# Tile-outermost order for a convolution layer, with its LayerNorm spread between the matmuls

## Chip, cores and metric

The program runs on the 8 cores of one Trainium2 chip. Each core works through two sequences of an encoder on its own; the cores exchange nothing. The metric is the device time of the slowest core in microseconds (us).

Some executions fall into a second, slower state in which the cores of one die, or of both, show a lower granted clock in the records; these last some per cent longer whatever the kernel.

Engines are named as in the profile: PE is the matrix engine (TensorE), PEld its weight loads, DVE is VectorE, ACT is ScalarE, POOL is GpSimd, SP the engine that issues most transfers.

## The reference

Four layers of mixer and MLP, each behind an RMS norm and added to x. The mixers are pooling, convolution, Fourier, pooling. Only the second one and the norm of the MLP behind it matter here:

```python
def conv_module(h, w_in, dw, dw_bias, ln_g, ln_b, w_out):
    val, gate = jnp.split(h @ w_in, 2, axis=-1)
    v = val * jax.nn.sigmoid(gate)                              # GLU, (B, S, 1024)
    v = lax.conv_general_dilated(v, dw[:, None, :], ...,        # depthwise over positions, width 31
        padding=((15, 15),), feature_group_count=D_CONV) + dw_bias
    mu = jnp.mean(vf, axis=-1, keepdims=True)                   # LayerNorm over the 1024 channels
    var = jnp.mean(jnp.square(vf - mu), axis=-1, keepdims=True)
    vn = (vf - mu) * lax.rsqrt(var + LN_EPS) * ln_g + ln_b
    return jax.nn.silu(vn) @ w_out

    # in the loop over layers
    x = x + mixers[i](rms_norm(x, norm_mix[i]))
    x = x + sq_relu_mlp(rms_norm(x, norm_mlp[i]), mlp_up[i], mlp_down[i])
```

A sequence has 2048 positions, cut into 4 tiles j of 512. The 1024 channels are 8 blocks c of 128.

## The kernel before

The kernel is a program generator: Python emits instructions in program order, and a recorder finds from the memory that each one touches which semaphores it must wait for. Memory is tracked in granules:

```python
GRAN = 128
...
        for l, h in zip(lo.tolist(), hi.tolist()):
            for gi in range(l // GRAN, (h - 1) // GRAN + 1):
                s.add((name, gi))
```

Two instructions that touch one granule are ordered if one of them writes, even where their bytes differ. Each engine is handed its instructions in program order, so "what stands where" is the whole schedule. An instruction that depends on an earlier one of its own engine waits on a semaphore too (PE excepted).

The convolution layer takes a channel block at a time. GLU of block c, then v goes to DRAM and comes back in four copies that are shifted by 8 positions, then four tiles of convolution, 32 matmuls each, on four column tiles of PE. The shifted copies are read for two tiles at once:

```python
        def glu(c, j):
            ...                                   # cut: 8 + 8 matmuls into banks bg, bv
            sg = SG.next()
            self.act(sg, bg, AF.Sigmoid)
            self.tt(Vc[c % 2][:, CONV_PAD + j * TT:CONV_PAD + (j + 1) * TT], bv, sg, ALU.mult)

        def vread(c, h, b):
            sc = self.scr["v"][c % 2]
            v4 = self.buf(b, BF16, (4, L))        # L: two tiles + 8
            for sh in (0, 2, 1, 3):
                src = bass.AP(sc.tensor, sc.offset + h * HT * TT + 8 * sh, [[VW, 32], [32 * VW, 4], [1, L]])
                self.dma("sp", f"v{c % 2}{h}", (s, c), v4[32 * sh:32 * sh + 32], src, ...)

        def conv(c, j, b, late=None):
            ...
            for m in range(8):
                for q in range(4):
                    self.mm(bank[32 * q:32 * q + 32, :], DG[:, q * 8 + m, :], ..., m == 0, m == 7, skip=True)
            self.act(C, bank, AF.Identity, bias=self.vcol(f"l{li}_conv_dw_bias", c))
            ...                                   # cut: C and its square are added up on VectorE over c
        for c in range(1, DC - 2):                # channel block outermost
            if c > 1:
                build_diag(c - 1)
                for j in range(NT):
                    glu(c, j)
            ...
            for h in range(2):
                for j in range(h * HT, (h + 1) * HT):
                    conv(c - 1, j, v4[h])
                spread(c, h, v4[h])               # write v of block c, read it back
```

All of LayerNorm and the output product therefore comes at the end, when the last channel block is done, and one tile stands behind the other:

```python
        def normalize(j, upto):
            for c in range(upto):
                ...
                self.tt(t1, Cv(c, j), ACC1[:, j, :], ALU.subtract, eng="pool" if c % 2 else "dve")
                self.tt(t1, t1, ACC2[:, j, :], ALU.mult)
                self.act(SLv(c, j), t1, AF.Silu, ...)

        def out(j, mid=None):
            ...
            for kc in range(DC):
                normalize(j, kc + 1)
                for oc in range(NB):
                    self.mm(banks[oc], wk(kc, oc), SLv(kc, j), kc == 0, kc == DC - 1)
            ...                                   # cut: x += bank, square of x for the next norm
        out(0, ...)
        self.x_ready(self.nxt, 0)
        out(3)
        self.x_ready(self.nxt, 3)
        self.slots_early(s, li, 1)
        self.h_open(self.nxt)
        self.h_step(99)                           # norm roots, 16 pieces and 16 differences for the MLP
        out(1)
        self.mlp_sums(s, li)
        out(2)
        for j in (1, 2):
            self.x_ready(self.nxt, j)
```

The MLP multiplies in a recursive form, on sums and differences of input pieces: tiles 0 and 3 are the first pair. Its first matmuls need the pieces of both, and so the root of the mean square of both.

## Time and profile before

| | before |
|---|---|
| time, first four runs | median 4682.6 us (4677.8 to 4897.6) |
| the six fast runs of the comparison below | 4677.8 to 4685.2 us |
| profiled execution, slowest core | 4678.4 us |
| cores, granted clock | 4667.3 to 4678.4 us, 0.971 |
| convolution layer, first / second sequence | 288.2 / 280.7 us |
| MLP behind it | 414.2 / 414.7 us |
| MLPs elsewhere | 392.6 to 414.1 us |

The lengths of stages run from the first matmul of a stage to the first of the next. I got them by counting the trace's matmuls off against the kernel's order of instructions; each is the median of the eight cores. On two cores of each trace some matmul records are missing; a recount on the six complete cores gives the same lengths within 1 us. The cores of one execution differ, by up to 4 us in a stage of the first sequence. Differences of about 1 us in the first sequence are therefore weak evidence.

A table load is what ACT does between functions of different sets; there are 17 in the program. `arena<-scr_v` is the shifted reload of v.

### The profile page before, as it was taken

To read this page: it belongs to the slowest core of one execution; us is meant where nothing else is said; L and a number is where in the kernel's file an instruction comes from. 1 tells how busy PE (TensorE), PEld (TensorE's weight loads), DVE (VectorE), ACT (ScalarE), POOL (GpSimd) and SP (SyncE) were. 2 spreads that over 40 slices of the span, in tenths; PEclk is the share of its full clock that TensorE was granted. 3 is DMA by queue.
4 is the path that set the end of the run, shared out by engine and by line. 5 is a ranking of instruction groups with operands and counts; after the bars stand their busy time and mean duration, and the time that the engine had idled before them with its cause. 6 is when DMAs were issued, how large, how long until landed. Compare 5 with 4: busy or idle time off the path is not lost.

```text
span 4678.4 us, 66415 instructions; the slowest of 8 cores (4667.3 to 4678.4 us)
## 1 busy us (share of the span) xinstructions
PE 4326.5 (92%) x21817; PEld 1964.7 (42%) x22222; DVE 2808.9 (60%) x5132; ACT 2003.5 (43%) x3367; POOL 158.7 (3%) x194
## 2 busy tenths in 40 slices
PE   7999987799978999999989999878999799999998
PEld 3444443344433444444444444433444344444443
DVE  2776645876647854578546556356646546526565
ACT  4533435433523445544355334344434245445334
POOL 0000001100020000000000000010000000000000
PEclk9999999899988999999999999988999899999999
DMA  6366653466634665267842443533444134413443
GB/s 152 85 161 203 165 127 84 91 163 203 176 112 106 177 193 142 70 162 203 232 142 97 156 146 118 137 75 125 151 149 150 51 131 153 151 59 112 156 178 131
DMA packets 97553, 652.07 MB, mean 139 GB/s; under 512 B 9920, under 2 KB 12096, under 8 KB 50368
## 3 DMA queue, kind: packets, MB, share of 16 engines
q1 hardware_dynamic: 77056, 517.25, 31.5%
q0 software_dynamic: 20160, 130.56, 15.8%
q8 instruction: 184, 3.01, 0.3%
q14 instruction: 153, 1.25, 0.1%
HBM read 625.08 MB, written 151.13 MB: 166 GB/s over the span
## 4 chain that ended last, share of the span: by engine, by line
PE 81%; DVE 7%; DMA 4%; issue 4%; ACT 3%; SPq 0%; DVEq 0%; POOL 0%; ACTq 0%; POOLq 0%
PE ps L330 81%; DVE arena L347 5%; ACT arena L344 3%; DVE arena L355 2%; DMA outT<-arena 1%; DMA scr_v<-arena 1%; DMA arena<-xT 1%; DMA arena<-l_pool_w_in 1%; DMA arena<-scr_v 0%; DMA arena<-l_pool_w_out 0%; DMA arena<-scr_mlp 0%; SPq L368 0%; ACT L344 0%; DVEq L282 0%; POOL arena L368 0%
## 5 line engine op out<-in xcount | busy, mean ns | idle before, releaser
L330 PE MATMUL ps<-arena 128*128 128x512 bf16 (+5 forms) x21817 | 4326.5, 374 | 333.3 <-DVE arena L347 112.7
L330 PEld LDWEIGHTS ps<-arena 128*128 128x128 bf16 (+1 forms) x22222 | 1964.7, 98 | 2694.7 <-issue 489.7
L347 DVE TENSOR_TENSOR arena<-arena,ps 128x512 f32<-128x512 f32 (+1 forms) x1090 | 726.0, 683 | 901.4 <-PE ps L330 886.8
L347 DVE TENSOR_TENSOR arena<-arena 128x512 bf16<-128x512 bf16 (+4 forms) x2364 | 1167.3, 512 | 165.8 <-ACT arena L344 128.0
L344 ACT ACTIVATE arena<-arena 128x512 bf16<-128x512 f32 (+3 forms) x1206 | 811.9, 681 | 671.8 <-DVE arena L347 625.7
L344 ACT ACTIVATE ps<-ps 128x512 f32<-128x512 f32 x768 | 447.0, 582 | 1107.6 <-PE ps L330 1046.9
L344 ACT ACTIVATE arena<-ps 128x512 f32<-128x512 f32 (+2 forms) x1112 | 613.2, 596 | 613.9 <-PE ps L330 573.8
L347 DVE TENSOR_TENSOR arena<-ps,arena 128x512 f32<-128x512 f32 (+1 forms) x584 | 401.3, 688 | 598.6 <-PE ps L330 555.0
L355 DVE SCALAR_TENSOR_TENSOR arena<-arena 128x512 bf16<-128x512 f32 (+1 forms) x960 | 669.0, 714 | 84.9 <-ACT arena L344 77.5
L344 ACT ACTIVATE arena<-ps,arena 128x512 bf16<-128x512 f32 (+2 forms) x264 | 168.7, 663 | 248.7 <-PE ps L330 208.1
L368 POOL DMA_DIRECT2D arena<-l_mlp x96 | 50.9, 530 | 1730.9 <-PE ps L330 1131.3
L351 DVE TENSOR_SCALAR arena<-arena 128x512 bf16<-128x512 f32 (+1 forms) x112 | 47.0, 462 | 73.8 <-DMA arena<-xT 50.6
L347 POOL TENSOR_TENSOR arena<-arena 128x512 f32<-128x512 f32 (+2 forms) x44 | 80.4, 1837 | 252.6 <-ACT arena L344 160.8
L344 ACT ACT_TABLE_LOAD x17 | 21.8, 1283 | 22.8 <-DMA arena<-xT 14.4
L368 POOL DMA_DIRECT2D arena<-l_conv_w_in x16 | 8.4, 531 | 676.2 <-DVE arena L347 522.6
L362 DVE COPY arena<-arena 128x512 f32<-128x512 f32 (+1 forms) x12 | 4.2, 346 | 39.9 <-ACT arena L344 39.9
L368 POOL DMA_DIRECT2D arena<-l_pool_w_in x14 | 7.5, 553 | 515.2 <-PE ps L330 514.0
L365 POOL MEMSET arena<- 128x1024 bf16 (+1 forms) x6 | 4.0, 702 | 419.6 <-PE ps L330 419.6
L368 POOL DMA_DIRECT2D arena<-l_conv_w_out x4 | 2.1, 527 | 237.4 <-PE ps L330 237.4
L368 POOL DMA_DIRECT2D arena<-l_pool_w_groupT x2 | 1.1, 535 | 90.4 <-DMA arena<-xT 52.4
L368 POOL DMA_DIRECT2D arena<-l_pool_w_out x4 | 2.1, 542 | 6.1 <-PE ps L330 6.1
L368 POOL DMA_DIRECT2D arena<-l_fourier_w_out_x x2 | 1.1, 554 | 0.0
(6 smaller groups left out, 2.0 us busy)
## 6 DMA issues: line engine op xcount, KB each, us to landing
arena<-scr_mlp SPq DMA_DIRECT2D x160, 1792.0 KB, 7.2
scr_mlp<-arena SPq DMA_DIRECT2D x64, 1792.0 KB, 6.5
arena<-l_mlp POOLq DMA_DIRECT2D x96, 1024.0 KB, 9.1
arena<-scr_v SPq DMA_DIRECT2D x128, 258.0 KB, 4.9
arena<-xT SPq DMA_DIRECT2D x32, 512.0 KB, 7.8
outT<-arena SPq DMA_DIRECT2D x16, 1024.0 KB, 5.3
arena<-l_conv_w_in POOLq DMA_DIRECT2D x16, 512.0 KB, 7.0
arena<-dfts SPq DMA_DIRECT2D x8, 1024.0 KB, 8.8
```

The costliest lines, as they stand in the source:

```text
L330: self.P.add("pe", lambda e: e.matmul(out, lhsT, rhs, start=start, stop=stop, skip_group_check=skip), reads=[lhsT, rhs], writes=[out])
L344: self.P.add("act", lambda e: e.activation(out, in_, func, **kw), reads=reads, writes=[out])
L347: self.P.add(eng, lambda e: e.tensor_tensor(out, in0, in1, op), reads=[in0, in1], writes=[out])
L351: self.P.add(eng, lambda e: e.tensor_scalar(out, in0, s1, None, op0), reads=reads, writes=[out])
L355: self.P.add(eng, lambda e: e.scalar_tensor_tensor(out, in0, scalar, in1, op0, op1), reads=reads, writes=[out])
L362: self.P.add(eng, lambda e: e.tensor_copy(out, in_), reads=[in_], writes=[out])
L365: self.P.add(eng, lambda e: e.memset(ap, val), writes=[ap])
L368: return self.P.add(q, lambda e: e.dma_start(out=out, in_=in_), reads=[in_] + list(reads), writes=[out] + list(writes), chan=chan, group=g ...
```

## The change

The intent is to keep PE fed through the whole layer. The loop is turned: position tile outermost, channel block inside, in the tile order 0, 1, 3, 2. So a tile's LayerNorm and output can lie beside GLU and convolution matmuls of the next tiles. The reload works a tile at a time with four slots read ahead. The LayerNorm sums of the last two tiles are made by PE in two banks of their own, one convolution late. The sigmoid becomes a tanh, because tanh shares ACT's table with silu (sigmoid(x) = (1 + tanh(x/2))/2; the half goes into the diagonals). The roots for the MLP are prepared piece by piece, squares of tiles 1 and 2 go into the MLP. Memory is tracked at 64 bytes.

The core of the diff, cuts marked with "...":

```diff
-GRAN = 128
+GRAN = 64
...
-    M[:, lay["mask"]:lay["mask"] + 32] = np.tile(np.eye(32), (4, 1))
+    M[:, lay["mask"]:lay["mask"] + 32] = 0.5 * np.tile(np.eye(32), (4, 1))
...
-            self.act(sg, bg, AF.Sigmoid)
-            self.tt(Vc[c % 2][...], bv, sg, ALU.mult)
+            self.act(sg, bg, AF.Tanh, scale=0.5)
+            self.stt(v, sg, 1.0, bv, ALU.add, ALU.mult)
...
+        order = [(c, j) for j in (0, 1, 3, 2) for c in range(DC)]
+        def vslot(k):
+            return self.buf(v4[k % 4 // 2], BF16, (4, L), (k % 2) * (BUFSZ // 2))
...
+            if k + 4 < len(order):
+                vread(k + 4)
...
+            if onpe:                       # tiles 3 and 2
+                sq, cb = SB[0].next(), SB[1].next()
+                self.act(sq, bank, AF.Square, bias=b)
+                silus()
+                self.copy(cb, C)
+                flush()                    # sums of the convolution before this one
+                late.append((j, c, cb, sq))
...
+        def ln(j, c, lag=False):
+            C = Cv(c, j)
+            self.tt(C, C, M[slot[j]], ALU.subtract, eng="pool" if j == 0 and c % 2 else "dve")
+            self.tt(C, C, R[slot[j]], ALU.mult)
+            lagged.append((j, c))          # the silu follows later
...
+        for c in range(DC):
+            conv(16 + c)
+            if c == 0:
+                ln_stats(1)
+            if c > 1:
+                ln(1, c - 2, True)
+        Cb[2] = self.take(6, 7)
+        conv(24)
+        ln_stats(3)
...
+        for c in range(1, DC):
+            conv(24 + c)
+            if c > 2:
+                ln(3, c - 3, True)
...
+        out(1, 0)
+        ln_stats(2)
+        self.rot = Rot([ps[:, i, :] for i in range(8)])
+        for c in range(DC - 3, DC):
+            ln(3, c)
+        for oc in range(1, DC):
+            out(1, oc)
+            ln(2, oc - 1)
+        ln(2, DC - 1)
...
+        first = [h[0]] + [h[2 + 8 * k + q] for k in range(4) for q in range(2)]
+        rest = [h[1]] + [h[2 + 8 * k + q] for k in range(4) for q in range(2, 8)]
+        for oc in range(DC):
+            out(3, oc)
+            first.pop(0)()                 # root of tile 0, then its pieces
+        self.htodo = first + rest
+        self.rot.i = 0
+        for oc in range(DC):
+            out(2, oc)
+            if oc > 0:
+                self.h_step(4)             # root of tile 3, the rest
         self.mlp_sums(s, li)
-        out(2)
+        nx.lazy = [1, 2]
```

## The prediction

> **What bounds the kernel now.** I read the page's head and its chain of work first, to see which engine sets the end.
>
> ```profile
> span 4678.4 us, 66415 instructions; the slowest of 8 cores (4667.3 to 4678.4 us)
> PE 4326.5 (92%) x21817; PEld 1964.7 (42%) x22222; DVE 2808.9 (60%) x5132; ACT 2003.5 (43%) x3367; POOL 158.7 (3%) x194
> PE 81%; DVE 7%; DMA 4%; issue 4%; ACT 3%; SPq 0%; DVEq 0%; POOL 0%; ACTq 0%; POOLq 0%
> ```
>
> TensorE carries 81% of the chain, so the other 19% are what a rescheduling can win. The diff touches the convolution layer, which each core runs twice (two sequences), and the head of the MLP after it. The second view is busy time by stretch, cut at those layers. Columns: stretch; busy us and count of PE, weight loads, DVE, ACT, POOL; granted clock; DMA share; GB/s.
>
> ```profile
> 172.00:568.00 396.00, 389.06 (x1763) 175.40 (x1798) 282.43 (x526) 171.02 (x300) 14.78 (x28) 1.00 0.66 176
> 568.00:740.00 172.00, 157.89 (x1298) 72.74 (x1314) 72.60 (x107) 57.89 (x89) 2.11 (x4) 0.97 0.58 133
> 740.00:761.00 21.00, 15.42 (x239) 7.32 (x233) 9.44 (x14) 13.72 (x21) 2.49 (x2) 0.92 0.58 130
> 761.00:856.00 95.00, 63.04 (x251) 25.79 (x257) 71.53 (x90) 47.78 (x56) 30.89 (x21) 0.86 0.09 16
> 856.00:880.00 24.00, 6.09 (x16) 1.57 (x14) 22.36 (x40) 7.45 (x9) 0.00 (x0) 0.57 0.37 71
> ...
> 3094.00:3181.00 87.00, 62.26 (x250) 25.34 (x254) 67.28 (x91) 47.34 (x55) 19.25 (x14) 0.86 0.10 36
> 3181.00:3205.00 24.00, 5.80 (x15) 1.49 (x14) 22.25 (x40) 7.37 (x9) 0.00 (x0) 0.63 0.27 102
> ```
>
> The MLP (172 to 568) is full. The convolution layer is not: its output part (761 to 856) keeps PE busy 63 of 95 us, and in the 24 us from 856 it does 16 matmuls while DVE is busy 22.4 us. The third view is what PE waited for from 568 to 880.
>
> ```profile
> PE ps L330 <- ACT arena L344: 30.5, 13, 9.3
> PE ps L330 <- DMA arena<-scr_v: 15.1, 4, 7.1
> PE ps L330 <- DVE arena L355: 12.7, 4, 4.0
> PE ps L330 <- DVE arena L347: 9.5, 4, 6.2
> ```
>
> ACT is the LayerNorm's silu at the end of subtract, multiply, silu; the DMA is the shifted reload of v before the first convolution; DVE L355 are the normed MLP inputs.
>
> The floor of a layer: full matmuls start 0.216 us apart in dense stretches, and a convolution (32 matmuls, four column tiles at a time) takes 1.73 us, read from start times (the timeline gives 3.65 us for 64 of them, with entry). Going into the tiled form and out costs 0.27 us together (0.10 on the full side, up to 0.17 on the other). The order of instructions gives 1802 matmuls per layer: 778 full x 0.216 = 168, 32 convolutions x 1.73 = 55.4, about 12 round trips x 0.27 = 3.2, plus 1.5 for the MLP's first: 228 us. The first layer with MLP head takes 312 us (568 to 880), the second 305 (2900 to 3205). Lost: 84 and 77, 161 in all, 3.4% of the kernel.
>
> **What the Trainium skill says.** "ScalarE activation tables: per-element evaluation and per-set limits", section "What a function is on this engine", puts two functions of different sets one table load of 1283 ns apart. The trace agrees: 17 loads, mean 1283 ns. "TensorE: Matmul & The Clock Gate", section "What's actually happening", says the clock halves after an idle window of about 3.4 us and recovers after as much work. The stretch table agrees in direction: clock 0.57 in the head, 1.00 in the MLP; so a long wait costs a little more than itself. "GPSIMD Engine Reference" lists GpSimd's SBUF interfaces as shared with VectorE, contended by DVE instructions with two SBUF inputs. The trace fits: such 128x512 f32 TENSOR_TENSORs average 809 ns (median 692) where GpSimd subtracts alongside. "DMA: Bandwidth & Descriptors", section "How a descriptor splits into AXI transactions", has unaligned descriptors fetch bytes that they don't use; the reload packets of 2064 B average 145 ns against 108 for 2048 B rows of the input.
>
> **The change part by part.**
> 1. The loop turns from channel block outermost to position tile outermost, with whole tiles of LayerNorm and output between GLU and convolution work. All eight GLUs of tile 1 separate the first reload from its use: the 7.9 and 12.6 us before the first convolutions, and 8.2 and 3.7 inside them, should go (32 us over both layers).
> 2. The LayerNorm of a tile is now spread under GLUs or convolutions. The stalls of the output part go, except around the statistics (below). GpSimd subtracts 4 times per layer, not 16.
> 3. LayerNorm sums of tiles 2 and 3 move from DVE to PE: 32 ones-matmuls instead of 4. Added PE per layer: 28 x 0.216 = 6.0, and about 12 more changes of form (the sums stand between convolutions) x 0.27 = 3.2. Together 9.3 per layer, 18.6 in all, all on the path. New floor 238.
> 4. Sigmoid becomes tanh in the silu's set. Ln and Exp still switch, and they are now spread out: the compiled program has 29 loads against 17, 6 more per layer x 1.28 = 7.7 us of ACT. They lie beside PE work except in the two statistics between back-to-back convolutions. There, one convolution with its sums takes PE 1.73 + 0.27 + 0.43 = 2.43 us, ACT 0.57 + 0.57 + 0.72 = 1.86 (spacing of such ACTIVATEs when dense), DVE 0.34 + 2 x 0.61 = 1.56. The statistics put square, copy, load, Ln, Exp, load (0.49 + 0.49 + 1.28 + 0.62 + 0.54 + 1.28 = 4.7 us) on ACT at once; PE, which waits each time for the sums of the convolution before, loses by my step-through 0.8 us at the first and 3.0 at the second.
> 5. The MLP head. The squares of x for tiles 0 and 3 move under the outputs, tiles 1 and 2 into the MLP, and half of the pieces that the first matmuls need are made early. What is left is DVE's queue after the last convolution: 4 LayerNorm chunks x 1.22 = 4.9; outputs of tile 1 with LayerNorm of tile 2, 8 x (0.60 + 1.22) = 14.6; outputs of tile 3 with squares and 7 pieces, 8 x 0.60 + 7 x 0.335 + 7 x 0.663 = 11.8; outputs of tile 2 with 9 pieces and 16 differences, 4.8 + 6.0 + 5.4 = 16.2. With about 3 us of start and a wait of 1.8 for the root of tile 3 it ends near 52 us, while PE has 24 x 1.73 + 1 = 43. So 8 us per layer stay; in the first sequence, where the slot sum now stands on DVE behind all this (GpSimd did it before), 9.7.
> 6. Weight slabs come earlier, and dependencies are tracked at 64 B. Outside the convolution layers and the MLP after them the PE, ACT and DVE order is unchanged; I count nothing.
>
> Sum per layer: floor 238; statistics 3.8; head 8.0 or 9.7; reloads 2; clock after these waits 3; unlisted 3. That makes 259.5 and 257.8 against 312 and 305: savings of 52.5 and 47.2, together 100 us. 4683 - 100 = 4583, 2.1% less.
>
> **The rivals.**
> DMA becomes the bound of the 16 back-to-back convolutions. Each needs 532 KB in 512 packets of 1040 B, 219 GB/s at 2.43 us, while the reload reached 230 to 240 GB/s at most in 4 us samples of the trace. If a packet costs in proportion to 2064 B at 145 ns, some 85 ns with a fixed part (estimate), a convolution's reads take 2.7 us on 16 engines, and the four slots read ahead nearly absorb it. If the cost is fixed per packet, 4.6 us, 20 to 25 us per layer are lost, and the kernel ends at 4625 to 4635. For it: twice the packets for the same bytes. Against it: the written packets of 1088 B took 68 ns.
>
> DVE bounds the tail more than I reckon: each microsecond there is on the path, and in-order waits for roots can add 5 per layer; then 4593.
>
> The rewrite hides nearly everything: with only the statistics and 5 us of tail left, 4560.
>
> ACT's extra loads come where PE waits on silu: 6 per layer, at worst 15 us in all, 4598.
>
> **Range and chances.** 2% is 4589, so the estimate sits 6 us beyond the line, while my sum of leftovers (42 us over both layers) may be half or double. Range 4556 to 4628. Chances: faster by over 2% 0.52, within 2% 0.47, slower 0.01: to be slower the added PE and a DMA bound would have to exceed all that is removed.
>
> **What would show it.** In stretches of the changed kernel: the first three quarters of the convolution layer near full PE with clock 1.00 (parts 1, 2); some 56 more weight loads (3); 29 table loads (4); PE waits on ACT of 3 to 5 us per layer among the convolutions; PE idle 8 to 10 us at the MLP's first matmuls with DVE full (5); PE waits on the reload of v under 3 us per layer. Wrong if those waits exceed 10 us per layer, if the head still costs 20, or if the MLP gets longer than 394 us past its head.

## More of the kernel before

The lines that show what bounds this kernel are in the prediction. Two more of the page are wanted later. The first is a group of instructions: line, engine, operation, count, then busy us and mean ns of one, then the idle time before them. The second is a transfer: what is written from what, count, KB each, and the median us from issue to landing.

```profile
L344 ACT ACT_TABLE_LOAD x17 | 21.8, 1283 | 22.8 <-DMA arena<-xT 14.4
...
arena<-scr_v SPq DMA_DIRECT2D x128, 258.0 KB, 4.9
```

## The result, and the profile after

| | before | after |
|---|---|---|
| fast runs of the comparison | 4677.8 to 4685.2 us (6) | 4602.0 to 4608.0 us (5) |
| ratio of fast runs | | 0.9836, 95% interval 0.9823 to 0.985 |
| median of all runs, slow ones included | 4862.3 us (15) | 4652.5 us (10) |
| profiled execution, slowest core | 4678.4 us | 4603.3 us |

A ratio is the mean time of one kernel's fast runs over that of the other's from the same rounds, so it is not quite the ratio of medians. The two medians of all runs hold different shares of slow runs and say nothing about the change. The kernel is 1.6% faster. The fast runs lie 19 to 25 us above the predicted 4583, inside the range; the saving is 75 us where 100 was predicted, and that puts the change within 2%, not beyond it.

The head of the page after:

```profile
span 4603.3 us, 67285 instructions; the slowest of 8 cores (4589.4 to 4603.3 us)
...
PE 4348.3 (94%) x22278; PEld 1962.0 (43%) x22278; DVE 2775.5 (60%) x5157; ACT 2019.4 (44%) x3425; POOL 115.2 (3%) x166
...
PE 85%; DVE 6%; DMA 3%; issue 3%; ACT 3%; SPq 0%; DVEq 0%; POOL 0%; ACTq 0%; POOLq 0%
...
L346 ACT ACT_TABLE_LOAD x29 | 37.2, 1283 | 25.9 <-DMA arena<-xT 14.0
...
arena<-scr_v SPq DMA_DIRECT2D x256, 130.0 KB, 3.7
```

PE's share of the chain rose from 81% to 85%. The 56 added weight loads and the 29 table loads are as reckoned. The reload has twice the transfers at half the size.

Busy time by stretch in the first sequence, core 4 (columns as in the prediction: stretch; PE, PEld, DVE, ACT, POOL; clock; DMA share; GB/s):

```profile
568.00:740.00 172.00, 167.79 (x1266) 74.38 (x1264) 82.92 (x128) 74.96 (x111) 5.45 (x5) 1.00 0.53 115
740.00:774.00 34.00, 27.12 (x378) 10.19 (x377) 18.54 (x33) 26.75 (x41) 0.57 (x1) 1.00 0.81 166
774.00:832.00 58.00, 43.97 (x196) 19.13 (x194) 49.10 (x87) 24.62 (x34) 1.05 (x2) 0.94 0.06 9
832.00:856.00 24.00, 23.38 (x96) 9.98 (x97) 18.08 (x36) 15.35 (x28) 0.53 (x1) 0.87 0.78 187
```

The part up to 740 us is now nearly full. From 740 to 774, the last of the 16 back-to-back convolutions, PE is busy 27 of 34 us, and ACT is nearly as busy. From 774 to 832, the outputs, PE is busy 44 of 58 us beside a DVE that is busy 49. What PE waited for, 568 to 840 us (us in total, times, longest):

```profile
PE ps L332 <- DVE arena L349: 15.1, 4, 8.3
PE ps L332 <- DVE arena L364: 4.9, 3, 1.7
PE ps L332 <- ACT arena L346: 2.8, 3, 1.7
PE ps L332 <- DMA arena<-scr_v: 2.7, 1, 2.7
```

And in the second sequence, 2862 to 3130 us:

```profile
PE ps L332 <- DVE arena L349: 14.4, 4, 8.3
PE ps L332 <- DVE arena L364: 4.9, 3, 1.7
PE ps L332 <- ACT arena L346: 2.8, 3, 1.7
```

The waits for ACT's silus and for the reload are nearly gone. DVE (L349: its two-input operations; L364: the copy of a convolution for the sums on PE) has taken their place. Where the time went, by stages (median of eight cores, us):

| stage | before | after | difference |
|---|---|---|---|
| convolution + MLP, first sequence | 288.2 + 414.2 | 264.1 + 393.9 | -24.1 - 20.4 = -44.5 |
| convolution + MLP, second sequence | 280.7 + 414.7 | 261.4 + 394.8 | -19.3 - 19.9 = -39.2 |
| Fourier + MLP, first sequence | 154.4 + 403.9 | 156.4 + 401.9 | 0.0 |
| last pooling + MLP, first sequence | 136.4 + 404.1 | 139.7 + 406.5 | +5.7 |
| Fourier + MLP, second sequence | 137.1 + 401.5 | 138.9 + 400.7 | +1.1 |
| last pooling + MLP, second sequence | 129.0 + 414.1 | 130.7 + 413.7 | +1.3 |

The changed layers save 83.7 us and other layers, which the diff does not touch, lose 8.1. (The recount gives 7.3; the MLP behind the last pooling layer of the first sequence, with its scatter of 4 us, is the uncertain part.)

The same gaps placed by the prediction's own terms (gaps of PE over 0.4 us, from the start of one matmul to the start of the next, on core 4; us per layer):

| place | predicted, first / second | first | second |
|---|---|---|---|
| silus of tile 0 before its first output | 0 | 2.5 | 2.5 |
| statistics of tile 1 | 0.8 | 0.6 + 1.9 | 0.5 + 1.9 |
| statistics of tile 3 | 3.0 | 1.2 + 2.0 + 2.0 | 1.2 + 2.0 + 2.0 |
| reload of v | 2 | 3.1 | 0 |
| head: output of tile 1, root of tile 3, MLP's first matmul | 9.7 / 8.0 | 1.2 + 8.6 + 5.8 | 1.3 + 8.6 + 5.2 |
| sum | 15.5 / 13.8 | 28.9 | 25.2 |

The gaps are 13.4 and 11.4 us longer than reckoned, the layers only 8.0 and 8.0 (52.5 - 44.5 and 47.2 - 39.2): the difference is 5.4 and 3.4. Each gap holds an ordinary spacing of 0.22 us, about 2 us per layer, so of the 6 us set aside for clock and unlisted losses some 3 and 1.5 were not used. The clock's part was used: after the gaps of 8.6 and 5.8 us in the first sequence, 6 and 12 matmuls start 0.43 us apart, twice the ordinary spacing, which is worth about 4 us. The wait for the reload in the first sequence varies, from 0.8 to 1.1 us on cores 1, 3 and 5 to 2.7 on core 4.

### The profile page after: what moved, and what is told of

The parts are those of the page before. It is cut to its first block, busy times and chain, and to the rows that moved or that the text cites. A ratio compares the mean times of both kernels' runs of the same rounds, so it can differ in the third digit from the quotient of the medians.

```text
span 4603.3 us, 67285 instructions; the slowest of 8 cores (4589.4 to 4603.3 us)
## 1 busy us (share of the span) xinstructions
PE 4348.3 (94%) x22278; PEld 1962.0 (43%) x22278; DVE 2775.5 (60%) x5157; ACT 2019.4 (44%) x3425; POOL 115.2 (3%) x166
## 3 DMA queue, kind: packets, MB, share of 16 engines
q14 instruction: 157, 1.29, 0.1%
## 4 chain that ended last, share of the span: by engine, by line
PE 85%; DVE 6%; DMA 3%; issue 3%; ACT 3%; SPq 0%; DVEq 0%; POOL 0%; ACTq 0%; POOLq 0%
PE ps L332 85%; DVE arena L349 4%; ACT arena L346 3%; DVE arena L357 2%; DMA outT<-arena 1%; DMA arena<-xT 1%; DMA arena<-l_pool_w_in 1%; DMA arena<-l_pool_w_out 0%; DMA arena<-scr_mlp 0%; DMA arena<-scr_v 0%; SPq L370 0%; DVEq L283 0%; ACT L346 0%; POOL arena L370 0%; DMA scr_v<-arena 0%
## 5 line engine op out<-in xcount | busy, mean ns | idle before, releaser
L349 DVE TENSOR_TENSOR arena<-arena,ps 128x512 f32<-128x512 f32 (+1 forms) x1090 | 729.6, 684 | 903.0 <-PE ps L332 895.2
L349 DVE TENSOR_TENSOR arena<-arena 128x512 bf16<-128x512 bf16 (+4 forms) x2368 | 1127.1, 494 | 125.7 <-ACT arena L346 85.8
L346 ACT ACTIVATE arena<-arena 128x512 bf16<-128x512 f32 (+3 forms) x1188 | 780.8, 665 | 659.6 <-DVE arena L349 621.9
L349 DVE TENSOR_TENSOR arena<-ps,arena 128x512 f32<-128x512 f32 x520 | 357.6, 688 | 471.4 <-PE ps L332 426.2
L346 ACT ACTIVATE arena<-ps,arena 128x512 f32<-128x512 f32 (+2 forms) x328 | 205.6, 667 | 223.8 <-PE ps L332 196.8
L357 DVE SCALAR_TENSOR_TENSOR arena<-arena,ps 128x512 bf16<-128x512 f32 x64 | 43.6, 686 | 104.3 <-PE ps L332 83.9
L346 ACT ACT_TABLE_LOAD x29 | 37.2, 1283 | 25.9 <-DMA arena<-xT 14.0
L349 POOL TENSOR_TENSOR arena<-arena 128x512 f32<-128x512 f32 (+2 forms) x16 | 37.0, 2330 | 256.1 <-ACT arena L346 180.0
L364 DVE CAST arena<-arena 128x512 bf16<-128x512 f32 x32 | 13.7, 428 | 36.0 <-ACT arena L346 35.9
L364 DVE COPY arena<-arena 128x512 f32<-128x512 f32 (+1 forms) x8 | 2.5, 306 | 7.7 <-ACT arena L346 7.7
```

The costliest lines, as they stand in the source:

```text
L346: self.P.add("act", lambda e: e.activation(out, in_, func, **kw), reads=reads, writes=[out])
L349: self.P.add(eng, lambda e: e.tensor_tensor(out, in0, in1, op), reads=[in0, in1], writes=[out])
L357: self.P.add(eng, lambda e: e.scalar_tensor_tensor(out, in0, scalar, in1, op0, op1), reads=reads, writes=[out])
L364: self.P.add(eng, lambda e: e.tensor_copy(out, in_), reads=[in_], writes=[out])
```

## The experiments

The theory that I took into the first runs: the head is DVE's queue, longer than reckoned because dependent pairs cost more and because it waits for roots; the 8 us in foreign layers are the position at which the PSUM banks' rotation is left behind; the rest of the convolution layer is statistics. The rivals are told with each run. Runs 4, 6, 7 and 8 have one fast execution each (4600.4, 4607.9, 4616.7 and 4627.5 us, the last with two cores at clock 0.974), so they are read by the lengths of their stages.

### 1. The bank rotation handed on

```diff
         nx.lazy = [1, 2]
+        self.rot.i = 2
```

The kernel takes PSUM banks in rotation. The convolution layer before left the counter at 2, the changed one at 1, and the layers after it start there.

> The changed kernel with one line more: the PSUM bank counter is set to 2 at the convolution layer's end, where the kernel before left it (the change leaves it at 1). Theory (bank phase): the Fourier and pooling layers, whose instructions did not change, became 1.7 to 3.3 us longer because their matmuls meet another bank's eviction; with the counter as before they return to their old lengths (154.4 / 136.4 / 137.1 / 129.0 us for the two Fourier and the two later pooling layers on the median core, from 156.4 / 139.7 / 138.9 / 130.7), some 6 to 8 us in all, ratio to before 0.9820. Rival (finer dependency tracking of 64 B changed waits everywhere): no effect, 0.9836.

Measured: Fourier and last pooling layers 154.5, 136.3, 137.3, 129.0 us, which are the lengths of the kernel before (154.4, 136.4, 137.1, 129.0); with their MLPs 7.7 us less than the changed kernel (6.7 by the recount, most of it in the last pooling layer of the first sequence). Fast runs 4597.6, 4599.1 and 4619.4 us (the last with two cores at clock 0.974 to 0.975); the interval of the ratio, 0.9841 (0.9779 to 0.9902), is too wide to show the 8 us by itself. The stage lengths settle it: a counter off by one costs layers that the diff does not touch about 8 us. The rival, the finer granule, is excluded by run 2, where these layers keep the changed kernel's lengths.

### 2. Memory tracked at 128 bytes again

```diff
-GRAN = 64
+GRAN = 128
```

> The changed kernel with dependencies tracked at 128 B again instead of 64 B. Theory (64 B matters only inside the new convolution layer, or not at all): Fourier and pooling layers stay at 156.4 / 139.7 / 138.9 / 130.7 us, convolution layers change by under 2 us. Rival (64 B tracking made the other layers longer): they return to 154.4 / 136.4 / 137.1 / 129.0 us.

Measured: ratio 1.0223 (1.0179 to 1.0267), slower than the kernel before. The profiled run had one die slow; on the other die the convolution layers take 90.6 and 87.0 us more and no other stage moves by more than the cores of one execution differ. The waits of PE from 568 to 930 us on core 0 of the undisturbed die:

```profile
PE ps L332 <- DMA arena<-scr_v: 71.8, 15, 8.8
```

One slot of the reload is half a buffer, 4160 bytes: 65 x 64, but 32.5 x 128. At 128 bytes two neighbouring slots share a granule, and the convolution that reads one waits for the reload that has just been issued into the other. The recorder's own dependencies say so: with 64 bytes convolution k waits for reload k alone, with 128 bytes convolution 1 waits for reload 4 too, 3 for 6, and so on. What the waits leave of the loss lies in slower matmuls between them (granted clock 0.84 from 740 to 850 us). So the finer granule, which I had counted as nothing, is what lets the new layer read ahead at all.

### 3. The root of tile 3 later

```diff
-        rest = [h[1]] + [h[2 + 8 * k + q] for k in range(4) for q in range(2, 8)]
+        rest = [h[2 + 8 * k + q] for k in range(4) for q in range(2, 8)]
...
+        self.sq_flush()
...
-            if oc > 0:
-                self.h_step(4)
+            if oc == 5:
+                self.h_step(1)
+                h[1]()
+            if oc > 5:
+                self.h_step(8)
+        self.h_step(99)
```

The largest single wait of PE, 8.6 us, stands at the ones-matmul of the root of tile 3. Either the root is the loss, or it is only the place where PE meets DVE's queue. The edit also puts the evictions of tile 2's first outputs in front of the pieces on DVE.

> The matmul for the root of tile 3, at which PE waits 8.6 us in the layer's tail, is moved behind the sixth output of tile 2; the square sum before it is flushed earlier. Theory (VectorE's queue sets the tail; PE's wait is a symptom): PE no longer waits there but waits as much longer at the MLP's first matmuls; only VectorE's own 2.5 us of idling for that root goes: convolution layer with MLP head 2 to 3 us shorter per layer. Rival (the in-order wait of PE is the loss): 7 to 9 us per layer.

Measured: the convolution layers are 9.7 and 10.0 us shorter and the MLPs 7.7 and 5.1 longer, so 2.0 and 4.9 us per layer are won. In the trace a stage ends where the MLP's first matmul starts, so most of the wait has moved over that border. The rival's 7 to 9 us did not come, so the queue theory holds, though the 4.9 is more than its 2 to 3. No ratio was formed: both runs that count as fast (4635.7 and 4639.4 us) have two cores at clock 0.967 to 0.968.

### 4. The root of tile 0 earlier

```diff
         out(1, 0)
         ln_stats(2)
+        self.root(nx, 0, self.RS[0])
...
-        first = [h[0]] + [h[2 + 8 * k + q] for k in range(4) for q in range(2)]
+        first = [h[2 + 8 * k + q] for k in range(4) for q in range(2)]
```

> The root of tile 0 is computed right after the last LayerNorm statistics (sharing their table) rather than behind the silus of tile 2. Theory (VectorE's queue sets the tail and its 3.1 us of idling for this root is on the path): 3 us shorter per layer, in the PE wait at the root of tile 3. Rival (ScalarE's silus set the tail): the two ACTIVATEs push the silus of tile 2 later and nothing, or less than 1 us, is won.

Measured: -1.3 and -0.8 us per layer, a miss for the theory and close to the rival. The trace shows where the 3.1 us went. In the first sequence PE's waits for DVE fall from 15.1 to 10.0 us, but those for ACT rise from 2.8 to 6.1: one of 3.2 us now stands before the third output of tile 1, where the changed kernel has none. Behind it DVE waits for PE (1.0 and 0.8 us), and for the root of tile 3 it waits 3.6 us instead of 2.5.

### 5. The tail rebuilt

```diff
         for c in range(DC):                    # among the convolutions of tile 3
             conv(16 + c)
             if c == 0:
                 ln_stats(1)
+                self.root(nx, 0, self.RS[0])
             if c > 1:
                 ln(1, c - 2, True)
+                first.pop(0)()                 # pieces of tile 0, in a free buffer
...
+            for q in todo.get(c, ()):          # all of ln(3, *) among the convolutions of tile 2
+                ln(3, q, True)
...                                             # outputs in the order 3, 1, 2; root of tile 3 after out(1, 3)
+        self.rot.i = 2
```

> VectorE's queue after the last convolution is shortened, no work is removed: the root and the 8 pieces of tile 0 and the last LayerNorm chunks of tile 3 are done among the convolutions (VectorE had about 0.7 us of slack in each of the 16), the outputs run in the order 3, 1, 2, the root of tile 3 stands behind the fourth output of tile 1; the bank counter as before. Theory (VectorE's queue sets the tail, 52 us of work against 42 of PE): with 9 us less in that queue the waits of 8.6 and 5.8 us shrink to under 4 together: 10 to 13 us per layer shorter than the changed kernel, plus 8 us for the bank counter: profiled span 4565 to 4575, ratio to before 0.976. Rival (VectorE is full among the convolutions already, since dependent pairs are slower than I reckoned): the time moves to the convolutions, under 4 us per layer won.

Measured: four fast runs of 4580.9 to 4585.2 us and a fifth of 4602.2 (one die at clock 0.976), ratio 0.9797 (0.9767 to 0.9828). Of this the handed-on rotation is 8 us; the layers themselves are 4.5 and 7.4 us shorter, not 10 to 13. The waits of the first sequence (568 to 832 us) show where it stopped:

```profile
PE ps L332 <- DVE arena L349: 8.5, 2, 7.8
PE ps L332 <- ACT arena L346: 6.6, 7, 1.9
```

One wait of nearly 8 us remains, at the MLP's first matmul, for an eviction of the last tile's outputs. Moving work in front of the last convolution shortened the queue, but not enough.

### 6. The sums of tile 3 back on DVE

```diff
-            onpe = j > 1
+            onpe = j == 2
...
-            if j > 1:
+            if j == 2:
```

> LayerNorm sums of tile 3 back on VectorE (tile 2 stays on PE). Theory (the move to PE pays because VectorE would bound these convolutions): PE has 5.6 us less to do in 8 convolutions, VectorE 8 x 1.2 more less the casts, 2.6 us per convolution against 1.9 of PE: convolution layer the same to 3 us longer than the changed kernel's 264 / 261 us. Rival (the added 9 us of PE are a plain loss): 4 to 6 us shorter.

Measured: +5.4 and +4.0 us per layer, more than the 0 to 3 expected. In the first sequence PE's waits for DVE go from 20.2 to 21.9 us and those for the reload from 2.7 to 7.0. That view counts a wait from the modelled end of a matmul. From start to start, PE's gaps over 0.4 us in the convolution layer grow by 9 to 13 us on four cores, and the rest of its time falls by 5 to 7. PE saves matmuls and loses more by waiting, so adding PE work here was right.

### 7. Sigmoid instead of tanh

```diff
-    M[:, lay["mask"]:lay["mask"] + 32] = 0.5 * np.tile(np.eye(32), (4, 1))
+    M[:, lay["mask"]:lay["mask"] + 32] = np.tile(np.eye(32), (4, 1))
...
-            self.act(sg, bg, AF.Tanh, scale=0.5)
-            self.stt(v, sg, 1.0, bv, ALU.add, ALU.mult)
+            self.act(sg, bg, AF.Sigmoid)
+            self.tt(v, bv, sg, ALU.mult)
```

> Sigmoid instead of tanh for the gate (another table set than silu's; 41 table loads compiled instead of 29, 6 more per layer). Theory (ScalarE has slack beside the GLUs, so loads count only where PE waits for silu at the first output of tile 0): 1 to 4 us longer per layer. Rival (the loads lie on the path): 6 x 1.28 = 7.7 us or more per layer.

Measured: +6.1 and +7.6 us per layer, with

```profile
L346 ACT ACT_TABLE_LOAD x41 | 52.6, 1283 | 40.4 <-DVE arena L349 17.1
```

Twelve loads more are 6 per layer, 7.7 us at 1.283 each, and the layers are longer by nearly that. I had expected the loads to lie beside PE work for the most part; that was wrong. Most of the loss stands in one place: in the first sequence PE's wait for the last silus before tile 0's first outputs grows from 1.7 to 6.0 us, and its waits for ACT from 2.8 to 7.5 in all. That every load is on the path is not shown; ACT waits for DVE between some of them.

### 8. Squares of tiles 1 and 2 in front of the MLP again

```diff
-        nx.lazy = [1, 2]
+        for j in (1, 2):
+            self.x_ready(nx, j)
```

> The square sums of tiles 1 and 2 at the end of the layer as in the kernel before, not inside the MLP. Theory (this is part of what the head of 20 us was): VectorE gets 2 x 2.2 us more in the queue that sets the MLP's first matmuls, and ScalarE 4 x 1.9 us: 4 to 8 us longer per layer. Rival (they run beside the MLP's start at no cost): under 1 us.

Measured: +1.2 and -0.8 us per layer, nothing; the theory of 4 to 8 missed and the rival was right. These squares come after everything that the MLP's start needs, so where they stand makes no odds here.

### 9. LayerNorm pairs taken apart

```diff
         for oc in range(1, DC):
             out(1, oc)
-            ln(2, oc - 1)
-        ln(2, DC - 1)
+            mul(2, oc - 1)
+            sub(2, oc)                  # of the next chunk
+            silus()
+        mul(2, DC - 1)
...                                      # the three chunks ln(3, 5..7) likewise
```

The prediction priced a LayerNorm chunk at 2 x 0.61 us. In the changed kernel's DVE timeline (start, duration, operation, tiles, count, and idle time before it if there was some) a chunk is a subtract and a multiply of the same tile, shown as "x2" behind each eviction:

```profile
783.13 1.48 DVE L349 TENSOR_TENSOR arena<-arena 128x512 f32<-128x512 f32 x2
784.53 0.68 DVE L349 TENSOR_TENSOR arena<-arena,ps 128x512 f32<-128x512 f32 x1
785.13 1.48 DVE L349 TENSOR_TENSOR arena<-arena 128x512 f32<-128x512 f32 x2
```

From the start of a pair to the next start is 1.40 us (784.53 - 783.13), of an eviction 0.60. So the multiply, which reads what the subtract wrote, starts 0.79 us after it.

> The changed kernel with one difference: in the tail after the last convolution, the subtract and the multiply of one LayerNorm chunk no longer follow each other directly on VectorE; the subtract of the next chunk (or an eviction) stands between them. Same instructions, same number. Theory (the prediction took 0.61 us for each of the two, but a 128x512 f32 pair in which the second reads what the first wrote is spaced 0.79 us, against 0.60 for independent neighbours): 11 chunks get 0.18 us shorter, VectorE's queue after the last convolution ends 2.0 us earlier, convolution layer plus MLP after it are 1.5 to 2.5 us shorter in each sequence. Rival (the queue waits for the roots on ScalarE anyway, so that what is saved before them turns into waiting): under 0.7 us per layer, though the spacing itself changes.

Measured: the profiled run had one die slow; on the other the layers are 1.6 us (262.5 + 394.1 against 264.1 + 394.1) and 2.3 us (259.6 + 394.3 against 261.4 + 394.8) shorter than the changed kernel on the same cores. The same stretch of the timeline, now with pairs that do not depend on each other:

```profile
782.65 1.29 DVE L349 TENSOR_TENSOR arena<-arena 128x512 f32<-128x512 f32 x2
783.85 0.68 DVE L349 TENSOR_TENSOR arena<-arena,ps 128x512 f32<-128x512 f32 x1
```

1.20 us for the same two instructions. The fast runs took 4596.0 and 4596.7 us (a third took 4618.9), and the ratio is 0.9834 (0.9803 to 0.9865). The theory holds: 2 us per layer of the missing 8 were this spacing. The ratio alone does not show it, as its interval holds the changed kernel's 0.9836.

### 10. The sums three convolutions behind

```diff
-                flush()
+                flush(keep=2)                  # keeps the sums of two convolutions back
...
+        SG = Rot(SG.items[:2])                 # room for four sum buffers each
+        SB = [Rot(SB[k].items + [self.buf(sgb, BF16, (TT,), 4096 + (2 * k + i) * 1024) for i in range(2)])
+              for k in range(2)]
```

What PE ran into at the statistics of tile 3 is seen in ACT's timeline of the changed kernel:

```profile
752.93 1.28 ACT L346 ACT_TABLE_LOAD   x1 [0.38 <-DVE arena L349]
754.22 1.45 ACT L346 ACTIVATE arena<-arena 128x512 f32<-128x512 f32 x2
755.58 1.25 ACT L346 ACTIVATE arena<-ps,arena 128x512 f32<-128x512 f32 x2
756.84 1.28 ACT L346 ACT_TABLE_LOAD   x1
758.14 1.52 ACT L346 ACTIVATE arena<-arena 128x512 bf16<-128x512 f32 x2
759.56 2.40 ACT L346 ACTIVATE arena<-ps,arena 128x512 f32<-128x512 f32 x4
```

Load, Ln and Exp, a convolution's two evictions, load back, two silus of tile 1 that I had not placed there, and only then the next convolution's evictions at 759.56, 6.6 us after the first load. DVE copies those and PE takes the copies into its sums, one convolution behind: it waited three times.

> The changed kernel with the ones-matmuls of a convolution's LayerNorm sums put behind the third convolution after it instead of the next (four buffers for each of the two summands instead of two). Same instructions. Theory (TensorE runs into ScalarE's backlog of 4.7 us of statistics because the sums stand only one convolution of 2.43 us behind): the waits of the changed kernel at the statistics of tile 3 (1.15 + 2.04 + 1.95 us) and the second wait at those of tile 1 (1.9 us) fall to under 1.5 us together, the convolution layer plus the MLP after it is 4 to 7 us shorter per sequence. Rival (the tail is set by VectorE's queue, which has its own backlog at that time): the waits go, but the MLP's first matmul waits that much longer, and convolution layer plus MLP together gain under 2 us.

Measured: the waits at the statistics of tile 3 are gone, and of tile 1's pair only 0.5 us is left. The second sequence is 3.8 us shorter, just under the 4 to 7 expected; the first 0.6, which is the rival's. What took the place in the first (735 to 770 us, core 7):

```profile
PE ps L332 <- DMA arena<-scr_v: 4.6, 3, 3.9
```

and the DMA beside it, first the changed kernel, then this one, 735 to 755 us (last two columns: DMA share, GB/s):

```profile
735.00:755.00 20.00, 19.15 (x272) 7.12 (x272) 13.44 (x24) 16.92 (x25) 0.00 (x0) 1.00 0.98 206
```

```profile
735.00:755.00 20.00, 19.76 (x282) 8.05 (x282) 12.79 (x23) 19.05 (x28) 0.57 (x1) 1.00 1.08 217
```

With PE full, the reload needs a convolution's 532 KB every 2.43 us, 219 GB/s, and 217 is what the queues move at a DMA share of 1.08, that is, with the 16 engines always busy; the changed kernel is close to it with 0.98. Part of what they move is a load of 1 MB that is told next. This was the prediction's DMA rival, and it is right at its edge. In the first sequence the MLP's first weight slot, 1 MB on GpSimd's queue, is issued at 752.6 us into this full DMA, since its buffer comes free with the diagonals of channel blocks 0 to 3. Ratio 0.9819 (0.9799 to 0.9839); fast runs 4594.3 to 4598.1 us.

### 11. All of it together

The rebuilt tail (5), the lag (10) and the pairs (9). Further:

```diff
-        self.rot.i = 0
+        self.rot = Rot([ps[:, i, :] for i in (0, 6, 2, 4, 1, 3, 5, 7)])   # banks the MLP needs first, first
         for oc in range(DC):
             out(2, oc)
...
+        while rest:                     # eight differences behind the last eviction
+            rest.pop(0)()
```

> The rebuilt tail of an earlier run (squares, root and eight pieces of tile 0 and all of tile 3's LayerNorm among the convolutions; outputs in the order of tiles 3, 1, 2), with the sums three convolutions behind, the LayerNorm pairs apart, the last outputs put in PSUM banks that the MLP takes later, the eight last difference pieces behind the last eviction, and the first slot's sums placed where VectorE waits for the root of tile 3. Theory (what is left of the loss is VectorE's queue and ScalarE's backlog, each moved off): 5 to 9 us per layer less than the rebuilt tail alone, so about 4562 to 4572 us in the fast state, ratio to the kernel before 0.975 to 0.977; the wait at the MLP's first matmul falls from 8.1 us to under 3. Rival (the first MLP units need the same pieces and evictions and only wait a few matmuls later): the wait splits over the first ten matmuls of the MLP and its sum stays over 6 us; time within 3 us of the rebuilt tail.

Measured: fast runs 4576.1, 4578.7 and 4581.0 us, ratio 0.9783 (0.9753 to 0.9813); 1.6 and 2.6 us per layer less than the rebuilt tail. Waits of the first sequence (568 to 840 us, core 6):

```profile
PE ps L332 <- DVE arena L349: 5.9, 3, 4.8
PE ps L332 <- DMA arena<-scr_v: 5.6, 2, 4.7
PE ps L332 <- ACT arena L346: 4.3, 5, 1.7
```

The rival was nearer: the wait at the MLP's start is still 4.8 us (under 3 was expected), and the full DMA claims its part. In the second sequence the queue is off the path (0.3 us for L349), and silus that come late for the first output take its place, 8.4 us of waits for ACT.

### 12. The slot load out of the way, and two outputs in front

Against run 11; cut from the diff: LayerNorm of tile 2 and the pieces stand an output earlier or later to fit.

```diff
-        dgb = self.take(4, 5)
+        dgb = self.take(5, 4)
...
-        out(3, 0)
+        out(1, 0)
         ln_stats(2)
         self.rot = Rot([ps[:, i, :] for i in range(8)])
+        out(1, 1)
+        out(3, 0)
```

> The previous best version with two differences. (1) The two buffers of the convolution's diagonals are swapped, so that the first weight slot of the MLP (1 MB on GpSimd's queue in the first sequence), which takes over the lower buffer, can only be loaded after the last convolution and no longer while the last reloads of v are under way. (2) The first two outputs of tile 1, whose silus are long done, come before the first output of tile 3, whose silus are late. Theory: (1) the wait of 4.7 us for the reload of v in the first sequence falls under 1 us and the second sequence, where that slot comes on the same queue behind the reloads, keeps its 0.5 us; (2) the waits for silus at the start of the outputs (2.2 us in the first sequence, 7.5 in the second) fall under 1.5 each; convolution layer and MLP after it together 4 to 7 us shorter in each sequence, the kernel at 4562 to 4570 us. Rival: VectorE's queue sets the end of the tail all the same, so each wait taken away comes back at the MLP's first matmuls: under 2 us per layer, 4573 to 4578 us.

Measured: in the first sequence (568 to 840 us)

```profile
PE ps L332 <- DVE arena L349: 6.1, 3, 4.8
PE ps L332 <- DVE arena L364: 5.6, 4, 2.5
PE ps L332 <- ACT arena L346: 3.1, 3, 1.7
...
PE ps L332 <- DMA arena<-scr_v: 0.3, 1, 0.3
```

The reload's wait fell from 5.6 to 0.3 us, and in the second sequence stayed as small (0.5 to 0.7): the slot load was its cause. The silus are off the path too, but the statistics of tile 2 now stand right behind the last convolution and PE waits there for the copies (L364). The wait of 4.8 us at the MLP's start in the first sequence stays. The layers are 2.5 and 4.5 us shorter than in run 11; only the second reaches the theory's 4 to 7. Fast runs 4574.1, 4576.6 and 4577.5 us, ratio 0.9765 (0.9716 to 0.9815). It is the fastest kernel of this study, against 4602.0 to 4608.0 for the changed kernel, in the rival's 4573 to 4578 and short of the 4562 to 4570 that I expected.

## Why the prediction was right or wrong

**The floor.** Right as a guide: of the 84 and 77 us per layer that it called lost, the change took back 44.5 and 39.2 although it adds PE work. Run 12, with the same arithmetic in another order, took back 8.7 and 14.5 us more (249.6 + 399.7 and 247.1 + 394.6 us).

**Part 1, reload stalls.** Right in mechanism: the 15.1 us of waits for the reload in the first sequence are 2.7 on core 4, and none are left in the second. That 2.7 is near the predicted 2 is luck: it falls while the load of the MLP's first slot is under way (issued at 760.0 us, landing 11.0 us later), which the prediction did not consider and to which run 12 traces the like wait of run 11. And two conditions went unseen. The finer granule is one: without it the layer loses 90 us (run 2). The other is that the new reload fills the DMA, so it has no slack for the slot load (runs 10 and 12).

**Part 2, LayerNorm under other matmuls.** Right for tiles 1 and 3. For tile 0 it was not complete: the last two silus before its first output cost 2.5 us per layer, which I did not list.

**Part 3, sums on PE.** The added instructions are as counted (56 more weight loads). Run 6 shows that they pay: without those of tile 3, each layer is 4 to 5 us longer. A change of form and back costs 0.22 us in the trace (see the last section), not 0.27, which makes the floor about 1 us too high.

**Part 4, statistics and tables.** This term failed in size: 3.8 us per layer predicted, 7.7 and 7.6 measured (6.6 and 6.5 without the ordinary spacings). The step-through counted Ln, Exp and two loads as ACT's backlog of 4.7 us, and left out two silus of tile 1 and a convolution's evictions that program order puts in between. The profile puts most of it down to DVE (L364, 4.9 us), whose copies wait for these evictions. Run 10 took exactly these waits away; in the second sequence, where PE waits 1.7 us for the reload and not 5.3, 3.8 us came back. The tanh was worth more than I said: run 7.

**Part 5, the MLP head.** The step that failed most, with the right mechanism: 9.7 and 8.0 us predicted, 15.6 and 15.1 measured. A small slip helped: 52 us of DVE less 43 of PE is 9, not the 8 that the sum used. DVE's queue was to end 52 us after the last convolution, and ended 59 us after it (773.5 to 832.3 us in the first sequence). The terms, worked out from the timeline of the changed kernel:

```profile
802.32 0.75 DVE L357 SCALAR_TENSOR_TENSOR arena<-arena 128x512 bf16<-128x512 f32 x1 [3.14 <-ACT arena L346]
...
817.31 1.41 DVE L357 SCALAR_TENSOR_TENSOR arena<-arena 128x512 bf16<-128x512 f32 x2 [2.48 <-ACT arena L346]
818.64 0.68 DVE L349 TENSOR_TENSOR arena<-arena,ps 128x512 f32<-128x512 f32 x1
819.24 1.81 DVE L349 TENSOR_TENSOR arena<-arena 128x512 bf16<-128x512 bf16 x4
```

A chunk takes 1.40 us, not 1.22: 12 chunks are 2.2 us. A bf16 difference takes 0.43 us in the queue (four from 819.24 to the next start at 820.97), not 0.335, as half of them depend on their predecessor (0.52 us after its start, the others 0.34): 16 are 1.5 us. DVE is idle 3.1 us for the root of tile 0, which I had not counted, and 2.5 instead of 1.8 us for the root of tile 3. That makes 7.5 us, against the 7 that were missing. Run 9 tests the first of these terms and run 4 the third; the other two are only read from the timeline. The Trainium skill, "VectorE: DVE Perf Modes", section "The DRAIN you can't avoid", says, from copies, that a semaphore after each operation costs nothing extra; here a pair in which the second waits for the first took 0.2 us longer than a pair that does not, and run 9 shows it in the length of the layers. Runs 3, 5 and 11 show that the queue and not the root as such is what PE meets; run 4 shows that removing the idle time for the root of tile 0 brings a wait for ACT instead.

**Part 6, "Outside ... I count nothing".** Wrong: 8 us. The order of instructions outside was indeed unchanged, but the PSUM banks that they use were not. Run 1 shows it by a one-line cure. I had compared orders of instructions, not operands.

**Sum.** 100 predicted, 75 found: 16 us in the changed layers (per layer, without the ordinary spacings: statistics about 3, head 5 to 6, silus 2, the reload +1 in the first sequence and -2 in the second, less the 3 and 1.5 of the reserve that were not needed) and 8 us outside.

**The rivals.** "DVE bounds the tail more" is what happened, and by a little more than its own 10 us; the in-order waits for roots were part of it. "DMA becomes the bound" in its milder form (85 ns a packet, nearly absorbed) is right: the 1040-byte packets took 76 ns in the mean, against the 145 ns of the 2064-byte ones. The harsher form is refuted. ACT's extra loads came in the number predicted; the waits on silus, 2.5 us per layer, go in that rival's direction, and six loads more per layer made them longer (run 7), but no run here shows that the six of the change make them. That the rewrite hides nearly everything (4560) was not so; run 12 at 4574 to 4578 comes nearest, by further changes.

What stays open: I have not shown why a bank rotation off by one costs the pooling and Fourier layers what it does, bank by bank, nor why a wait of 4.8 us stays at the MLP's start in the first sequence of the fastest kernel.

## What to carry to other kernels

When work moves under other work, step the taking engine's queue through in program order with everything that stands in it, and price pairs that depend on each other from a pair in the trace, not from the average spacing. Compare the operands too (PSUM banks, buffers, granules): a rotation counter moved 8 us here, and the old granule would have cost 178. And expect the next bound right behind: DVE's queue, ACT's statistics and the reload of this layer lay within a few us of each other, so taking one away alone paid 0.6 to 5 us each time and all together 23.

## What the Trainium skill lacked or had wrong

- "VectorE: DVE Perf Modes", section "The DRAIN you can't avoid": it reports, for copies, that a semaphore after each costs nothing extra. For two 128x512 f32 operations the runs show 1.40 us where the second waits for the first and 1.20 where it does not.
- "ScalarE: Activation LUTs", section "What ACT_TABLE_LOAD costs": it puts every switch of sets at about 2.66 us in total, drain included. Here the next ACTIVATE starts 1.29 to 1.30 us after the load's start (752.93 to 754.22, 756.84 to 758.14), and the second load starts as the ACTIVATE before it ends (755.58 + 1.25 us, 756.84), so the load's 1283 ns are about the whole price.
- "TensorE: Matmul & The Clock Gate", section "Back-to-back issue gap": it gives about 131 ns per matmul at N=512 as the sustained figure and about 216 as that of a single one. The dense stretches here, with a weight load for each matmul, hold 0.216 us, at a granted clock of 1.00.
- "DMA: Bandwidth & Descriptors": the section on how a descriptor splits counts transactions for unaligned reads but gives no times. For the shifted reload the traces show 76 ns in the mean for 1040 bytes (52 in the median) and 145 ns for 2064.
- "TensorEngine Tiling (Array Packing)", section "Key Properties": it says that a change of tiling mode drains the engine, and gives no figure. In these traces the first matmul after a change starts 0.31 us after the one before it, either way, and not 0.22; going into the column-tiled form and back costs 0.22 us together, with 1.73 us counted for the convolution itself.
